# One rotation of four PSUM buffers for attention, in a hybrid encoder layer on one core

## The chip, the cores and the metric

The kernel runs on one core of one Trainium2 chip. The core has five engines with an instruction queue each: TensorE (PE in the profile, with its weight loads as PEld), VectorE (DVE), ScalarE (ACT), GpSimd (POOL) and SyncE (SP), which here only issues transfers. Matrix products and transposes run on TensorE and land in PSUM, which has eight banks of 2 KB for each of 128 partitions; a full tile of 128 x 512 float32 fills one. VectorE and ScalarE read PSUM. The metric is the device time of one execution in microseconds; less is better.

## The reference

The kernel computes one layer of an encoder on 2048 positions of width 1024, in float32. The input is normalised (RMS norm) and projected by `w_in` into 11 slots of 256 columns. Four mixers read them, each with a gate, and `w_out` projects their outputs back onto the residual:

```
h = rmsnorm(x, norm_g)
a_u, a_v, a_g, b_q, b_k, b_v, b_g, c_in, c_g, d_q, d_g = split(h @ w_in, 11)
y_a = chunked_spatial_gating(a_u, a_v, ...) * silu(a_g)     # 128x128 mixing per chunk
y_b = neighbourhood_attention(b_q, b_k, b_v, ...) * silu(b_g) # windows of 8 x 16 on a 32 x 64 grid, 4 heads
y_c = fourier_mixing(c_in, fn_w) * silu(c_g)                  # 2-D DFT, real part, then a linear map
y_d = memory_attention(d_q, rmsnorm(mem), ...) * silu(d_g)    # 256 memory tokens, 4 heads
x   = x + concat(y_a, y_b, y_c, y_d) @ w_out
```

## The kernel before

**Products.** To keep float32 accuracy at the faster rate, each operand is split into a high and a low half (`hi`, `lo`, type float32r): ScalarE copies the value with rounding (L506 and others), VectorE or GpSimd subtracts (L507 and others). A product then takes three matmuls, high by high, high by low and low by high. So a tile that leaves PSUM through `evac_split` is read twice: by the cast (L506) and, after that, by the subtraction (L507).

**Order.** TensorE's order is the program's: it is built by `drive`, which runs a filler (the projections, later the output projection) and squeezes in steps of other tasks as they fall due by a clock of costs that `mm` and `tr` add up. The instructions of the other engines and the transfers are ordered by Tile's own scheduler when the program is built; `hp(8000)` raises the priority of what is issued under it. Tile also sets all waits. On the chip every engine's queue runs in order.

**PSUM.** Eight banks: four in the pool `ps_acc` for the projections' sums, two in `ps_sc` and two in `ps_mi`. A pool's tiles take its buffers in rotation, whichever became free first by the scheduler's reckoning. A tile's first matmul waits until the last reader of the buffer's earlier tile has ended.

**Who uses the two small pools.** `ps_sc` (tiles `sc`): scores of both attentions, the sums of the memory's keys and values (`mem_kv`, L442), the Fourier sums (`acc`, L743), and an extra projection at the start. `ps_mi` (tiles `mi`): all else. That is transposes of normalised q and k (`emit_T`, read by L506/L507, or by L389/L390 where k is scaled), transposes of P (L592, L902) and the products with v (L600, L915) of both attentions, chunk mixing (`do_a`, L653), the first products of the Fourier stage (`pa`, L747), its two tiny products `pu` of two columns each (L773), and small preparations (`constants_a`: the bias; `constants_c`: the matrices G; `bcast`: the transposed norm rstd).

**Attention.** `pipeline` interleaves units. In step n it issues the score of unit n, the transposes of unit n-2, and, where unit n-3 closes an item, that item's product with v. An item of the memory attention (`d_`) has one unit, so a step takes three tiles: a score, a transpose tile and a product. An item of the window attention (`b_`) has two units, so two steps take five tiles. Between them the driver puts projection matmuls. A score of the memory attention is read by the row maximum (L575) and then by two exponentials (L579); a score of the window attention by one VectorE operation that adds the bias and takes the maximum (L886). P is scaled by VectorE (L583, L891) before it is transposed.

**Stages in time.** Start, with c_in and d_q and the memory's keys and values, up to some 100 us; memory attention of the first half of the positions among projections; projections alone; the Fourier stage among projections of the second half, from 347 us on; window attention, memory attention of the second half and both again, among the last projections and the output projection, from 472 us on; the rest of the output projection to the end.

Of the kernel before, what the change touches and what calls it, by code (L numbers as in the profile page):

```python
# [47 lines left out]
class Kern:  # L48
    def __init__(self, ctx, tc, ins, out, dbg=None):
        self.tc = tc  # L50
        self.nc = tc.nc
        self.ins = ins
        self.out = out
        self.ctx = ctx
        self.dbg = dbg
        p = lambda name, bufs, **k: ctx.enter_context(tc.tile_pool(name=name, bufs=bufs, **k))
        self.const = p("const", 1)
        self.xw = p("xw", 32)
        self.raw = p("raw", 5)
# [225 lines left out]
    def bcast(self, h):  # L285
        nc = self.nc
        ps = self.ps_mi.tile([8, 128], F32, name="mi")
# [79 lines left out]
    def transpose_pairs(self, srcs):  # L367
        ps = self.ps_mi.tile([128, 512], F32, name="mi")
# [71 lines left out]
    def mem_kv(self):  # L440
        nc, I = self.nc, self.ins
        ps = [self.ps_sc.tile([128, 512], F32, name="sc") for _ in range(2)]  # L442
        for k in range(8):
            with self.hp(0):
# [12 lines left out]
                w = [wt[:, k % 2, 0], wt[:, k % 2, 1]]  # L457
# [16 lines left out]
        for t in range(2):  # L474
# [7 lines left out]
                                    in1=self.vm[:, t, :, 0:HD].bitcast(F32), op=ALU.subtract)  # L482
        self.head_norm(q)
# [4 lines left out]
    def mem_k(self, twice):  # L488
        nc = self.nc
        self.km = [self.c([128, 4, 256], f"km{i}", F32R) for i in range(2)]  # L490
        for pr in range(2):
            ps = self.ps_mi.tile([128, 2, 256], F32, name="mi")
# [73 lines left out]
    def d_score(self, h, b, pr, hh, dq, o, ctx):  # L566
        nc = self.nc
        dqr = dq.bitcast(F32R)
        sc = self.ps_sc.tile([128, 512], F32, name="sc")
# [17 lines left out]
    def d_trans(self, h, b, pr, hh, dq, o, ctx):  # L587
# [4 lines left out]
        pt = self.ps_mi.tile([128, 2, 256], F32, name="mi")  # L592
# [5 lines left out]
    def d_pv(self, h, b, pr, hh, dq, o, ctx):  # L598
        PT = ctx["PT"][:, hh]
        pv = self.ps_mi.tile([128, 256], F32, name="mi")  # L600
# [9 lines left out]
    def constants_a(self):  # L610
# [10 lines left out]
        ps = self.ps_mi.tile([128, 512], F32, name="mi")  # L621
# [11 lines left out]
    def do_a(self, h, u, ps):  # L633
# [17 lines left out]
        for b in range(2):  # L651
            with self.hp(8000):
                ps2 = self.ps_mi.tile([128, 2, 2, 128], F32, name="mi")  # L653
# [10 lines left out]
    def constants_c(self):  # L664
# [7 lines left out]
        ps = self.ps_mi.tile([128, 4, 128], F32, name="mi")  # L672
# [3 lines left out]
        for pr in range(2):  # L676
            for i in range(2):
                nc.vector.tensor_copy(out=self.Gc[i][pr], in_=ps[:, pr * 2 + i, :])

    def fft(self, pool):  # L680
        nc, I = self.nc, self.ins
        for pr in range(2):
# [19 lines left out]
        for ty in range(4):  # L702
# [40 lines left out]
            acc = [self.ps_sc.tile([128, 512], F32, name="sc") for _ in range(2)]  # L743
            abs_ = {}
            for j in range(5):
                if j < 4:
                    pa = self.ps_mi.tile([128, 512], F32, name="mi")  # L747
# [24 lines left out]
            for pr, al in enumerate(als):  # L772
                pu = self.ps_mi.tile([128, 512], F32, name="mi")  # L773
                self.mm(pu[:, 0:2], self.Gc[0][pr], al[:, 2:4], True, True)
                nc.vector.tensor_copy(out=ucol[:, pr, :], in_=pu[:, 0:2])
# [12 lines left out]
            else:  # L788
                for pr in range(2):
# [14 lines left out]
                    nc.sync.dma_start(out=self.O[4 + pr][ty // 2], in_=z)  # L804
        self.done.add("fft")
# [65 lines left out]
    def b_score(self, pool, kv, qq, R, head, cb, ui, rb, gs, ctx):  # L871
# [5 lines left out]
        sc = self.ps_sc.tile([128, 512], F32, name="sc")  # L877
# [16 lines left out]
    def b_trans(self, pool, kv, qq, R, head, cb, ui, rb, gs, ctx):  # L894
# [7 lines left out]
        pt = self.ps_mi.tile([128, 4, 128], F32, name="mi")  # L902
# [6 lines left out]
    def b_pv(self, vt, R, head, cb, units, ctx):  # L909
# [5 lines left out]
        pv = self.ps_mi.tile([128, 2, 2, 128], F32, name="mi")  # L915
# [87 lines left out]
    def proj(self, h, *which):  # L1003
# [4 lines left out]
        for i, w in enumerate(which):  # L1008
            ps = []
            if i:  # L1010
                ps = [self.ps_sc.tile([128, 512], F32, name="sc") for _ in range(2)] + \
                     [self.ps_mi.tile([128, 512], F32, name="mi") for _ in range(2)]
            pss.append(ps)
            gens.append(self.slot(h, cs[w], w in self.NATURAL, ps, 1 if len(which) > 1 else 2))
# [32 lines left out]
    def main(self, P, es):  # L1047
# [7 lines left out]
        warm = self.ps_mi.tile([128, 512], F32, name="mi")  # L1055
# [51 lines left out]
    def run(self):  # L1107
# [6 lines left out]
        with tc.manual_schedule(engines={mybir.EngineType.PE}):  # L1114
            with ExitStack() as es:
# [4 lines left out]
                self.att = P("att", 2)  # L1120
                self.drive(self.main(P, es))

# [97 lines left out]
```

## Time and profile before

| | |
|---|---|
| median of 3 runs | 886.07 us (886.05 to 886.48) |
| the profiled execution | 886.93 us |
| its span, first to last instruction | 884.7 us |
| TensorE busy | 854.8 us, 97% of the span |
| VectorE, ScalarE, GpSimd busy | 516.5, 407.4 and 302.7 us |
| granted TensorE clock, mean | 0.993 of full speed |

Busy times are of one profiled execution. The profile names an instruction by its source line; most matmuls go through two helpers, so L135 is any matmul and L139 any transpose, and the tile (`mi`, `sc`, `acc`) tells which. Idle time of an engine is put down to what ended it.

### The profile page before, as it was taken

To read this page: it belongs to the slowest core of one execution; us is meant where nothing else is said; L and a number is where in the kernel's file an instruction comes from. 1 tells how busy PE (TensorE), PEld (TensorE's weight loads), DVE (VectorE), ACT (ScalarE), POOL (GpSimd) and SP (SyncE) were. 2 spreads that over 40 slices of the span, in tenths; PEclk is the share of its full clock that TensorE was granted. 3 is DMA by queue.
4 is the path that set the end of the run, shared out by engine and by line. 5 is a ranking of instruction groups with operands and counts; after the bars stand their busy time and mean duration, and the time that the engine had idled before them with its cause. 6 is when DMAs were issued, how large, how long until landed. Compare 5 with 4: busy or idle time off the path is not lost.

```text
span 884.7 us, 13646 instructions
## 1 busy us (share of the span) xinstructions
PE 854.8 (97%) x4448; PEld 714.5 (81%) x4448; DVE 516.5 (58%) x1104; ACT 407.4 (46%) x930; POOL 302.7 (34%) x329
## 2 busy tenths in 40 slices
PE   8999999999899999999999899999999999999998
PEld 7987788888688878787789788788877888878886
DVE  4345565487532646774444875776898877743331
ACT  5674354466732524443324544656775444521110
POOL 2136321155132213561231733442656333221110
PEclk9999999999999999999999999999999999999999
DMA  8958543455942653559668897864688987546662
GB/s 259 343 190 254 168 133 121 115 142 147 263 141 96 214 179 84 154 171 269 180 217 277 270 279 234 266 214 139 194 289 245 334 245 215 175 141 197 215 198 74
DMA packets 147462, 177.88 MB, mean 201 GB/s; under 512 B 29232, under 2 KB 105152, under 8 KB 147392
## 3 DMA queue, kind: packets, MB, share of 16 engines
q1 hardware_dynamic: 145104, 170.33, 62.1%
q0 software_dynamic: 1728, 6.29, 2.5%
q8 instruction: 35, 0.57, 0.3%
q10 hardware_dynamic: 560, 0.40, 0.2%
q14 instruction: 35, 0.29, 0.1%
HBM read 132.92 MB, written 44.05 MB: 200 GB/s over the span
## 4 chain that ended last, share of the span: by engine, by line
PE 67%; DMA 7%; DVE 6%; POOL 3%; issue 3%; ACT 2%; SPq 0%; DVEq 0%; POOLq 0%; ACTq 0%
PE acc L135 53%; PE mi L135 5%; PE sc L135 5%; PE mi L139 4%; DMA G<-st 2%; POOL hss L113 1%; DMA nat<-in_x 1%; DMA O<-sa_o 1%; DMA raw<-in_xT 1%; DMA qq<-QB 1%; DMA raw<-in_w_in 1%; DVE nat L364 1%; DVE PT L507 1%; DVE P L891 1%; DVE st L390 1%
## 5 line engine op out<-in xcount | busy, mean ns | idle before, releaser
L135 PE MATMUL acc<-hilo 128*128 128x512 f32 (+1 forms) x2880 | 709.9, 390 | 5.4 <-DVE nat L351 1.5
L135 PEld LDWEIGHTS acc<-hilo 128*128 128x128 f32 x2880 | 511.1, 189 | 96.7 <-ACT nat L353 1.6
L207 POOL TENSOR_TENSOR hilo<-raw,hilo 128x512 fp32r<-128x512 f32 x52 | 69.5, 1339 | 181.1 <-ACT hilo L205 160.6
L219 POOL TENSOR_TENSOR hilo<-raw,hilo 128x512 fp32r<-128x512 f32 x32 | 42.9, 1342 | 118.1 <-ACT hilo L217 94.6
L217 ACT CAST hilo<-raw 128x512 fp32r<-128x512 f32 x64 | 39.7, 621 | 75.7 <-PE acc L135 67.8
L953 POOL TENSOR_TENSOR nat<-nat 128x256 f32<-128x256 f32 x39 | 31.3, 805 | 104.2 <-DMA nat<-O 73.1
L507 DVE TENSOR_TENSOR PT<-mi,PT 128x512 fp32r<-128x512 f32 (+2 forms) x96 | 61.2, 637 | 8.1 <-ACT PT L506 8.1
L139 PE MATMUL mi<-ident,P 128*128 128x128 f32 (+1 forms) x352 | 54.6, 274 | 8.4 <-DVE PT L507 6.8
L139 PEld LDWEIGHTS mi<-ident,P 128*128 128x128 f32 (+1 forms) x352 | 42.2, 136 | 24.1 <-DVE PT L507 10.8
L959 ACT CAST hilo<-nat 128x256 fp32r<-128x256 f32 x64 | 25.7, 407 | 77.0 <-PE acc L135 67.3
L506 ACT CAST PT<-mi 128x512 fp32r<-128x512 f32 (+2 forms) x96 | 52.1, 542 | 18.9 <-PE mi L139 18.6
L888 ACT ACTIVATE P<-P,smx 128x288 f32<-128x288 f32 (+1 forms) x64 | 39.8, 622 | 40.3 <-DVE smx L886 40.1
L205 ACT CAST hilo<-raw 128x512 fp32r<-128x512 f32 x51 | 31.5, 619 | 48.3 <-PE acc L135 33.9
L219 DVE TENSOR_TENSOR hilo<-raw,hilo 128x512 fp32r<-128x512 f32 x32 | 23.7, 741 | 40.0 <-ACT hilo L217 34.1
L113 POOL TENSOR_TENSOR hss<-hss,mhalf 128x8 f32<-128x8 f32 x25 | 43.3, 1736 | 1.5
L891 DVE TENSOR_SCALAR P<-P,smx 128x288 f32<-128x288 f32 (+1 forms) x64 | 41.3, 645 | 1.9
L960 DVE TENSOR_TENSOR hilo<-nat,hilo 128x256 fp32r<-128x256 f32 x64 | 29.8, 474 | 21.4 <-ACT hilo L959 21.4
L579 ACT ACTIVATE P<-sc,smx 128x256 f32<-128x256 f32 x64 | 29.7, 469 | 23.4 <-DVE smx L575 23.2
L331 DVE TENSOR_TENSOR st<-acc,rbc 128x512 f32<-128x512 f32 x32 | 21.9, 683 | 30.2 <-PE acc L135 29.4
L928 POOL TENSOR_TENSOR ob<-tmp 64x128 f32<-64x128 f32 x64 | 30.3, 492 | 26.4 <-DVE tmp L924 25.4
L886 DVE CUSTOM_DVE_ANT_0 P<-sc,bt 128x288 f32<-128x288 f32 (+1 forms) x64 | 35.5, 555 | 3.1 <-PE sc L135 1.3
L126 DVE SCALAR_TENSOR_TENSOR hilo<-raw,gcol,hilo 128x512 fp32r<-128x512 f32 x32 | 25.2, 796 | 18.6 <-ACT hilo L125 18.2
(158 smaller groups left out, 1039.7 us busy)
## 6 DMA issues: line engine op xcount, KB each, us to landing
raw<-in_w_in SPq DMA_DIRECT2D x119, 256.0 KB
raw<-in_xT SPq DMA_DIRECT2D x32, 256.0 KB
nat<-in_x SPq DMA_DIRECT2D x32, 256.0 KB
G<-st SPq DMA_DIRECT2D x32, 256.0 KB
nat<-G SPq DMA_DIRECT2D x64, 128.0 KB
st<-in_x SPq DMA_DIRECT2D x32, 256.0 KB
out_y<-st SPq DMA_DIRECT2D x31, 256.0 KB
tab<-in_dft_s POOLq DMA_DIRECT2D x12, 512.0 KB, 4.3
```

What stands on the lines that cost most here:

```text
L113: nc.gpsimd.tensor_tensor(out=out, in0=out, in1=self.mhalf[:, :n], op=ALU.pow)
L135: self.nc.tensor.matmul(out=out, lhsT=lhsT, rhs=rhs, start=start, stop=stop, **k)
L139: self.nc.tensor.transpose(out=out, in_=in_, identity=self.ident)
L205: nc.scalar.copy(out=w[0], in_=raw)
L207: eng.tensor_tensor(out=w[1], in0=raw, in1=w[0].bitcast(F32), op=ALU.subtract)
L217: nc.scalar.copy(out=w[0], in_=raw)
L219: eng.tensor_tensor(out=w[1], in0=raw, in1=w[0].bitcast(F32), op=ALU.subtract)
L506: self.nc.scalar.copy(out=hi, in_=src)
L507: (eng or self.nc.vector).tensor_tensor(out=lo, in0=src, in1=hi.bitcast(F32), op=ALU.subtract)
L886: nc.vector.tensor_tensor_reduce(out=P[:, :n], in0=sc[:, :n], in1=bt[:, :n], op0=ALU.add, op1=ALU.min, scale=-1.0, scalar=3e38, accum_out= ...
L888: nc.scalar.activation(out=P[:, :n], in_=P[:, :n], func=AF.Exp, bias=sm[:, 1:2], scale=-1.0, accum_out=sm[:, 2:3])
L891: nc.vector.tensor_scalar(out=P[:, :n], in0=P[:, :n], scalar1=sm[:, 3:4], scalar2=None, op0=ALU.mult)
```

## The change

`psum()` closes the two small pools and opens others in their banks: either the two of two buffers, or one of four, which both names then stand for. It is called with the shared form at the end of `mem_kv`, with the split form at the start of the Fourier stage, and with the shared form again at its end. The new pools wait tile by tile (`reuse_waits="tile"`). All tiles of the small pools go by it, so `emit_T` and `do_a` too take from the four while these are shared. The two tiny products of the Fourier stage write columns 0:2 and 2:4 of one tile and are copied at once. The addition of the bias and the four copies of G are issued at higher priority.

```
-        self.ps_sc = p("ps_sc", 2, space=PSUM)
-        self.ps_mi = p("ps_mi", 2, space=PSUM)
+        self.pst = None
+
+    def psum(self, shared):
+        if self.pst is not None:
+            self.pst.close()
+        self.pst = ExitStack()
+        p = lambda name, bufs: self.pst.enter_context(
+            self.tc.tile_pool(name=name, bufs=bufs, space=PSUM, reuse_waits="tile"))
+        if shared:
+            self.ps_sc = self.ps_mi = p("ps_w", 4)
+            self.nsc = self.nmi = "w"
+        else:
+            self.ps_sc, self.ps_mi = p("ps_sc", 2), p("ps_mi", 2)
+            self.nsc, self.nmi = "sc", "mi"
...
     def mem_kv(self):
...
+        self.psum(True)
         self.head_norm(q)
...
     def constants_a(self):
...
-        nc.vector.tensor_tensor(out=self.bias2, in0=pv, in1=self.bias2, op=ALU.add)
+        with self.hp(8000):
+            nc.vector.tensor_tensor(out=self.bias2, in0=pv, in1=self.bias2, op=ALU.add)
...
     def constants_c(self):
...
-        for pr in range(2):
-            for i in range(2):
-                nc.vector.tensor_copy(out=self.Gc[i][pr], in_=ps[:, pr * 2 + i, :])
+        with self.hp(8000):
+            for pr in range(2):
+                for i in range(2):
+                    nc.vector.tensor_copy(out=self.Gc[i][pr], in_=ps[:, pr * 2 + i, :])

     def fft(self, pool):
         nc, I = self.nc, self.ins
+        self.psum(False)
...
-            for pr, al in enumerate(als):
-                pu = self.ps_mi.tile([128, 512], F32, name="mi")
-                self.mm(pu[:, 0:2], self.Gc[0][pr], al[:, 2:4], True, True)
-                nc.vector.tensor_copy(out=ucol[:, pr, :], in_=pu[:, 0:2])
+            if als:
+                pu = self.ps_mi.tile([128, 512], F32, name=self.nmi)
+                for pr, al in enumerate(als):
+                    self.mm(pu[:, pr * 2:pr * 2 + 2], self.Gc[0][pr], al[:, 2:4], True, True)
+                nc.vector.tensor_copy(out=ucol.rearrange("p a b -> p (a b)"), in_=pu[:, 0:4])
...
+        self.psum(True)
         self.done.add("fft")
...
                 self.att = P("att", 2)
+                self.psum(False)
                 self.drive(self.main(P, es))
+                self.pst.close()
```

Everywhere else the change only replaces a tile's name, `name="sc"` by `name=self.nsc` and `name="mi"` by `name=self.nmi`.

## Rows read from the trace of the kernel before

**Rows 1.** The page's first part: each engine's busy time, share and instructions

```profile
PE 854.8 (97%) x4448; PEld 714.5 (81%) x4448; DVE 516.5 (58%) x1104; ACT 407.4 (46%) x930; POOL 302.7 (34%) x329
```

**Rows 2.** Waits of TensorE: waiter, releaser, us in total, times, longest

```profile
PE mi L139 <- DVE PT L507: 8.1, 6, 1.9
```

**Rows 3.** Timeline, first half's memory attention: start, us, instruction, [idle before <-releaser]

```profile
220.93 0.46 ACT L579 ACTIVATE P<-sc,smx 128x256 f32<-128x256 f32 x1
...
223.56 0.66 PE L139 MATMUL mi<-ident,nat 128*128 128x128 f32 x4 [1.31 <-DVE PT L507]
...
225.63 0.74 PE L135 MATMUL mi<-PT,vm 128*128 128x256 f32 x4 [1.42 <-DVE st L390]
...
234.65 0.63 PE L139 MATMUL mi<-ident,P 128*128 128x128 f32 x4 [1.41 <-DVE st L390]
```

**Rows 4.** Timeline, Fourier stage

```profile
366.49 0.15 DVE L775 COPY ucol<-mi 128x2 f32<-128x2 f32 x1
...
366.69 0.38 PE L135 MATMUL mi<-al,G 128*128 128x2 f32 x2 [1.36 <-DVE ucol L775]
...
368.18 1.09 PE L139 MATMUL mi<-ident,nat 128*128 128x128 f32 x4 [0.30 <-DVE ucol L775]
```

**Rows 5.** Windows: length, engines' busy us (x), granted clock, DMA share, GB/s

```profile
367.00:372.00 5.00, 4.70 (x17) 3.63 (x17) 3.22 (x10) 1.80 (x5) 0.00 (x0) 0.66 0.63 204
```

**Rows 6.** Timeline, start of the window attention

```profile
474.94 0.44 PE L135 MATMUL sc<-kk,qq 128*128 128x384 f32 x1 [1.08 <-DVE smx L886]
...
475.79 0.37 DVE L891 TENSOR_SCALAR P<-P,smx 128x288 f32<-128x288 f32 x1
```

**Rows 7.** Timeline, window attention, a little later

```profile
494.19 0.35 DVE L891 TENSOR_SCALAR P<-P,smx 128x288 f32<-128x288 f32 x1
...
497.21 0.68 DVE L507 TENSOR_TENSOR PT<-mi,PT 128x512 fp32r<-128x512 f32 x1
...
497.94 0.53 PE L139 MATMUL mi<-ident,P 128*96 128x128 f32 x3 [1.31 <-DVE PT L507]
...
501.98 1.08 PE L135 MATMUL mi<-PT,vt 128*128 128x512 f32 x5 [1.68 <-DVE PT L507]
```

**Rows 8.** Timeline of TensorE, three stalls of the later attention

```profile
600.14 0.66 PE L139 MATMUL mi<-ident,P 128*128 128x128 f32 x4 [0.87 <-DVE PT L507]
...
674.08 0.66 PE L139 MATMUL mi<-ident,P 128*128 128x128 f32 x4 [0.80 <-DVE PT L507]
...
775.32 0.66 PE L139 MATMUL mi<-ident,P 128*128 128x128 f32 x4 [1.88 <-DVE PT L507]
```

**Rows 9.** Timeline, second half's window attention

```profile
663.99 0.64 PE L139 MATMUL mi<-ident,P 128*96 128x128 f32 x4 [1.94 <-DVE PT L507]
...
665.67 0.74 DVE L960 TENSOR_TENSOR hilo<-nat,hilo 128x256 fp32r<-128x256 f32 x2
```

**Rows 10.** Windows around it: PE, PEld, DVE, ACT, POOL busy, clock, DMA share

```profile
590.00:690.00 100.00, 96.16 (x504) 79.75 (x503) 80.27 (x174) 67.19 (x164) 53.17 (x54) 0.98 0.73 230
664.00:669.00 5.00, 4.87 (x19) 3.63 (x19) 3.96 (x11) 3.68 (x9) 4.89 (x5) 0.66 0.94 291
```

**Rows 11.** Timeline of TensorE, a product of the window attention

```profile
566.88 1.09 PE L135 MATMUL mi<-PT,vt 96*128 96x512 f32 x5 [0.62 <-DVE PT L507]
```

**Rows 12.** Timeline, the start of the kernel

```profile
70.05 0.66 PE L139 MATMUL mi<-ident,nat 128*128 128x128 f32 x4 [1.02 <-DVE G L678]
...
71.72 0.47 DVE L453 SCALAR_TENSOR_TENSOR P<-dq,gmcol,P 128x256 fp32r<-128x256 f32 x1
...
72.59 0.27 PE L139 MATMUL mi<-ident,rstd 128*8 128x128 f32 x1 [1.19 <-DVE bias L624]
```

**Rows 13.** Timeline, second half's memory attention

```profile
593.43 0.63 PE L135 MATMUL sc<-km,dq 128*128 128x256 f32 x4
...
597.95 0.63 PE L135 MATMUL sc<-km,dq 128*128 128x256 f32 x4
...
598.08 0.46 ACT L579 ACTIVATE P<-sc,smx 128x256 f32<-128x256 f32 x1
```

More of the change, by code (lines that the diff above doesn't have):

```diff
@@ L286, in bcast @@
         nc = self.nc
-        ps = self.ps_mi.tile([8, 128], F32, name="mi")
+        ps = self.ps_mi.tile([8, 128], F32, name=self.nmi)
         self.tr(ps, self.rstd[h])
@@ L367, in transpose_pairs @@
     def transpose_pairs(self, srcs):
-        ps = self.ps_mi.tile([128, 512], F32, name="mi")
+        ps = self.ps_mi.tile([128, 512], F32, name=self.nmi)
         for pr in range(2):
@@ L441, in mem_kv @@
         nc, I = self.nc, self.ins
-        ps = [self.ps_sc.tile([128, 512], F32, name="sc") for _ in range(2)]
+        ps = [self.ps_sc.tile([128, 512], F32, name=self.nsc) for _ in range(2)]
         for k in range(8):
@@ L491, in mem_k @@
         for pr in range(2):
-            ps = self.ps_mi.tile([128, 2, 256], F32, name="mi")
+            ps = self.ps_mi.tile([128, 2, 256], F32, name=self.nmi)
             for hh in range(2):
@@ L568, in d_score @@
         dqr = dq.bitcast(F32R)
-        sc = self.ps_sc.tile([128, 512], F32, name="sc")
+        sc = self.ps_sc.tile([128, 512], F32, name=self.nsc)
         for j in range(2):
@@ L591, in d_trans @@
         PT = ctx["PT"][:, hh]
-        pt = self.ps_mi.tile([128, 2, 256], F32, name="mi")
+        pt = self.ps_mi.tile([128, 2, 256], F32, name=self.nmi)
         for mt in range(2):
@@ L599, in d_pv @@
         PT = ctx["PT"][:, hh]
-        pv = self.ps_mi.tile([128, 256], F32, name="mi")
+        pv = self.ps_mi.tile([128, 256], F32, name=self.nmi)
         for mt in range(2):
@@ L620, in constants_a @@
         yield 12.0
-        ps = self.ps_mi.tile([128, 512], F32, name="mi")
+        ps = self.ps_mi.tile([128, 512], F32, name=self.nmi)
         pv = ps[:, 0:256].rearrange("p (a q) -> p a q", a=2)
         self.s_mix(pv, lnb)
-        nc.vector.tensor_tensor(out=self.bias2, in0=pv, in1=self.bias2, op=ALU.add)
+        with self.hp(8000):
+            nc.vector.tensor_tensor(out=self.bias2, in0=pv, in1=self.bias2, op=ALU.add)
         nc.vector.tensor_scalar(out=self.bias2, in0=self.bias2, scalar1=2.0, scalar2=None, op0=ALU.mult)
@@ L652, in do_a @@
             with self.hp(8000):
-                ps2 = self.ps_mi.tile([128, 2, 2, 128], F32, name="mi")
+                ps2 = self.ps_mi.tile([128, 2, 2, 128], F32, name=self.nmi)
                 for j in range(2):
@@ L671, in constants_c @@
         yield 10.0
-        ps = self.ps_mi.tile([128, 4, 128], F32, name="mi")
+        ps = self.ps_mi.tile([128, 4, 128], F32, name=self.nmi)
         for pr in range(2):
@@ L742, in fft @@
             yield 5.0
-            acc = [self.ps_sc.tile([128, 512], F32, name="sc") for _ in range(2)]
+            acc = [self.ps_sc.tile([128, 512], F32, name=self.nsc) for _ in range(2)]
             abs_ = {}
@@ L746, in fft @@
                 if j < 4:
-                    pa = self.ps_mi.tile([128, 512], F32, name="mi")
+                    pa = self.ps_mi.tile([128, 512], F32, name=self.nmi)
                     for pr in range(2):
@@ L876, in b_score @@
         gl = slice(r0 // 4 - (0, 3)[R], (r0 + nr) // 4 - (0, 3)[R])
-        sc = self.ps_sc.tile([128, 512], F32, name="sc")
+        sc = self.ps_sc.tile([128, 512], F32, name=self.nsc)
         q = qq[:, (rb - 2 * R) * 4 + cb, :]
@@ L901, in b_trans @@
         PT = ctx["PT"]
-        pt = self.ps_mi.tile([128, 4, 128], F32, name="mi")
+        pt = self.ps_mi.tile([128, 4, 128], F32, name=self.nmi)
         for s, gg in enumerate(gs):
@@ L914, in b_pv @@
         PT = ctx["PT"]
-        pv = self.ps_mi.tile([128, 2, 2, 128], F32, name="mi")
+        pv = self.ps_mi.tile([128, 2, 2, 128], F32, name=self.nmi)
         mms = [(pv, units[0][1][s], PT[:ck, s]) for s in range(2)]
@@ L1010, in proj @@
             if i:
-                ps = [self.ps_sc.tile([128, 512], F32, name="sc") for _ in range(2)] + \
-                     [self.ps_mi.tile([128, 512], F32, name="mi") for _ in range(2)]
+                ps = [self.ps_sc.tile([128, 512], F32, name=self.nsc) for _ in range(2)] + \
+                     [self.ps_mi.tile([128, 512], F32, name=self.nmi) for _ in range(2)]
             pss.append(ps)
@@ L1054, in main @@
         self.constants_mem()
-        warm = self.ps_mi.tile([128, 512], F32, name="mi")
+        warm = self.ps_mi.tile([128, 512], F32, name=self.nmi)
         for i in range(18):
```

## The prediction, as it was put on record

> **What bounds the kernel now.** I read the page's first part first: TensorE counts as busy for 97% of the span, no other engine for more than 58% [rows 1]. So time can only be won where TensorE stands still, and next I read who it waits for. The largest entry is waits of transposes into `mi` (L139) for the second half of a split (L507 on VectorE), 8.1 us in 6 waits [rows 2]. A transpose doesn't read what L507 writes, it reads P or a projection. One that waits for L507 waits for a buffer: two `mi` tiles are alive, and neither has been read to its end. Products do read what L507 writes, so each of their waits has to be looked at. Third, I went through the timeline around each stall and asked: was the data there earlier, and would another buffer have been free?
>
> **The change, part by part.** No matmul is added, removed or moved: TensorE's order is the program's, written out by the driver, and the change leaves its costs as they are. VectorE loses one tiny copy of 0.15 us [rows 4], which is worth nothing by itself. What changes is which earlier tile a tile has to wait for, and VectorE's order in two places. The prices below are the idle time that the timeline prints behind a matmul.
>
> *Memory attention of the first half.* Three stalls of 1.31, 1.42 and 1.41 us [rows 3]. The first and third are transposes, so they wait for buffers. The second is a product; it waits for L390, which it never reads, so for a buffer too. At the first of them both score buffers had been read to the end, the last one by an exponential that ended at 220.93 + 0.46 = 221.39. Sharing four should remove all three: 4.1 us. What follows is projection work whose loads are released by buffers that TensorE frees, so I keep the whole amount.
>
> *Fourier stage.* The second tiny product waits 1.36 us for the copy of the first (L775), and the next transposes wait 0.30 us for the second copy [rows 4]. With one buffer for both no product waits. The transposes then need the one copy, which in the trace would be over at 366.49 + 0.15 = 366.64, while they start at 368.18 now. I take 1.5 of the 1.66 us. The stall has a second price: right behind it the granted clock is 0.66 over 5 us [rows 5], that is at its lower level (1.2 GHz) for most of them. Lost: 0.34 x 5 = 1.7 us. If TensorE doesn't stand still there, I expect no fall: 1.7 us more.
>
> *Start of the window attention.* The third score waits 1.08 us for a score buffer [rows 6]. Four buffers remove that, but next in line is a transpose of P, scaled from 475.79 on in 0.37 us, so ready at 476.16, however early the score is. I take 0, bound 1.1. A little later a transpose waits 1.31 us and a product 1.68 us [rows 7]. The product's own data was there at 497.21 + 0.68 = 497.89, four us before it started; it is held by a buffer. Both go: 3.0 us.
>
> *Later attention.* Three transposes wait 0.87, 0.80 and 1.88 us for a buffer [rows 8]. The first and third I take whole; at the second VectorE is late in general, so 0.6. A fourth waits 1.94 us, but the output projection behind it needs the halves that L960 writes from 665.67 on [rows 9], and VectorE is busy 80.27 of 100 us around there [rows 10]. If the transpose starts earlier, the projection stands still instead. I take 0.3 us (bounds 0 and 1.94), and no credit for the lower clock that follows (0.66 over 5 us [rows 10], 1.7 us again). Sum: 0.87 + 1.88 + 0.6 + 0.3 = 3.6. One product waits 0.62 us for L507 of its own unit [rows 11]: that is data, and it stays.
>
> *Higher priority for two sets of VectorE operations at the start.* Transposes wait 1.02 us for the copies of G, and the transpose of rstd 1.19 us for the bias [rows 12]. Earlier copies free both, but the product behind the second one, to the memory's keys and values, needs the half that L453 writes from 71.72 on in 0.47 us, so at 72.19; the transpose starts at 72.59. That makes 0.4 us to be won, bounds 0 and 2.2.
>
> *Switching pools* three times issues nothing. A tile of a new pool waits at most for the last reader of its bank; I take 0, and as upper bound one wait like that of [rows 11] each, 1.9 us.
>
> Together 4.1 + 1.5 + 1.7 + 3.0 + 3.6 + 0.4 = 14.3 us. Part of it will be given back: a TensorE that comes earlier meets VectorE's data where it met a buffer before. The nearest row for that is the product that waits for its own data [rows 11]; four more of these are 2.4 us (bounds: 0, and the 6.6 us of the window attention's two terms, which is the first rival). That leaves some 12 us. The sum is made against the span of 884.7 us and that execution's own 886.93, which lies 0.86 above the median of 886.07: 874.9 for such an execution, 874.0 for the median.
>
> The Trainium skill, Perfetto Trace Analysis, section Identifying Performance Opportunities, says that the same gap repeating on the engine that should be saturated can mean too little PSUM for the next tile. Read that way, all of these stalls would go, which is the second rival below. The trace agrees only in part: the stalls are scattered over 700 us, and in some of them VectorE's data is late as well [rows 9].
>
> **Rivals.** *VectorE is what is late (0.18).* In the window attention the buffers may only be the place where its lateness shows; the waits then go over to data. For it: 80 of 100 us busy [rows 10]. Against it: P of the first transpose in [rows 7] was ready at 494.19 + 0.35 = 494.54, 3.4 us before the transpose started. Left are the terms before the window attention: 4.1 + 1.5 + 1.7 + 0.4 = 7.7, so 878.4.
>
> *Everything goes (0.10).* 8.1 [rows 2] + 1.68 [rows 7] + 1.42 + 1.41 [rows 3] + 1.66 [rows 4] + 1.08 [rows 6] + 2.21 [rows 12] = 17.6, with twice 1.7 of lost clock 21.0: 865.1. Against it stands the order of data in [rows 6, 9, 12].
>
> *DMA takes the lead back (0.08).* In places the transfers are close to saturation (a share of 0.94 [rows 10]). If TensorE's lead ends there and only the last stall of [rows 8] counts, the gain is 1.9: 884.2, hardly to be told from no change. Against it: most loads wait for buffers that TensorE frees, so they move with it.
>
> *Slower (0.06): scores hold the rotation up.* A score tile is read until its second exponential ends. In the second half's memory attention that is from 593.43 to 598.08 + 0.46 = 598.54, 5.1 us [rows 13]. The next score comes at 597.95, so a step is 4.5 us. Now the score's buffer is needed again two steps later, after 9.0 us; in a rotation of four with three tiles to a step, after 4/3 steps, 6.0 us. The margin is 0.9 us. If a new order on VectorE and ScalarE makes these reads later than that, transposes and products wait for scores. Over 80 units (16 to the memory, 64 windows) it decides from 0.18 us each, which eats the 14.3; at 0.3 us the time is 886.07 + 24 - 14.3 = 895.8. In this way the change could also fail to do what it says: which buffer a tile gets is fixed when the program is built, and on the chip that one may be the late one.
> The Trainium skill, TensorE: Matmul & The Clock Gate, section A second HAM failure mode: psum-queue depth-cycling, tells of short idle times between groups that cycle through PSUM banks, and of a clock that falls between them. Here the lower clock stands behind two stalls [rows 5, 10], and the change makes stalls fewer; in the slow case it would add to the loss.
>
> **How the numbers follow.** Forecast 874.0 with a chance of 0.58 (868 to 877 for itself). The range for 8 in 10 is 866 to 881: it takes in VectorE's case, the bounds of the forecast's own terms and the near side of the fast one, and leaves out DMA's case, the slow one and the far ends. About 0.2%, 1.8 us, is what a measurement of this kernel can tell from no change. Faster has the forecast, VectorE's and the fast case and a part of DMA's: 0.88. Same: 0.06. Slower: 0.06.
>
> **What would show it.** Right: in the memory attention of the first half TensorE waits for no buffer; the copy of the tiny products is there once, with no lower clock behind it; TensorE's waits at shared tiles fall from 17.1 us (the 17.6 without the score, with the 0.62) to under 6. The step on VectorE is right if the output projection waits for L960 near where the fourth transpose waited. Wrong: waits of TensorE for readers of scores (L579, L886), waits for L507 before products in place of those before transposes, or new stretches at the lower clock.

## The result, and the profile after

The changed kernel takes 876.97 us (median of 6 runs, 874.57 to 879.69); the kernel before takes 886.28 in the same measurement. The ratio is 0.9896, 95% interval 0.987 to 0.9922: 9.3 us less, with 6.9 to 11.5 inside the interval. The forecast was 874.0, 12 us less, range 866 to 881. A second program whose instructions stand in the same order (the fourth experiment) gave 878.25, ratio 0.9913 (0.9883 to 0.9943).

The profiled execution took 879.69 us with a span of 877.5, the longest of the six; before's took 886.93 with 884.7. So the two traces differ by 7.2 us, and it is these 7.2 that can be followed. The first part of the page after, which answers to [rows 1]:

```profile
PE 852.0 (97%) x4448; PEld 713.3 (81%) x4448; DVE 515.3 (59%) x1103; ACT 407.6 (46%) x930; POOL 302.0 (34%) x329
```

TensorE runs the same 4448 matmuls in the same order, so each can be found in both traces. Its start before minus its start after is the *lead* at that place. The forecast column adds up the prediction's terms.

| after the stalls of | start before | start after | lead | forecast |
|---|---|---|---|---|
| the head (transpose of rstd) | 72.59 | 72.44 | 0.15 | 0.4 |
| first half's memory attention | 234.65 | 229.20 | 5.45 | 4.5 |
| the projection behind it | 247.44 | 246.00 | 1.44 | 4.5 |
| Fourier stage | 371.19 | 366.97 | 4.22 | 7.7 |
| start of the window attention | 504.64 | 497.84 | 6.80 | 10.7 |
| later attention | 775.32 | 765.90 | 9.42 | 14.3 |
| output projection | 858.75 | 851.36 | 7.39 | 12.0 |

Stage by stage the wins are not far from the forecast's (5.3, 2.8, 2.6 and 2.6 us where it had 4.1, 3.2, 3.0 and 3.6). The lead is lost in two places that the forecast didn't name: the third row and the last.

*First half.* Timeline of TensorE after. The first three rows answer to [rows 3]:

```profile
221.37 0.60 PE L151 MATMUL w<-ident,nat 128*128 128x128 f32 x4
221.72 0.72 PE L147 MATMUL w<-PT,vm 128*128 128x256 f32 x4
...
229.20 0.60 PE L151 MATMUL w<-ident,P 128*128 128x128 f32 x4
...
234.10 0.71 PE L147 MATMUL w<-PT,vm 128*128 128x256 f32 x4 [1.12 <-DVE st L402]
...
243.26 1.66 PE L147 MATMUL acc<-hilo 128*128 128x512 f32 x6 [1.14 <-DVE st L343]
246.00 1.19 PE L147 MATMUL acc<-hilo 128*128 128x512 f32 x4 [1.07 <-DVE st L343]
```

The three stalls of before have no bracket any more: no wait. They gave 1.47, 1.72 and 1.54 us of lead. Behind them stand three new ones, which cost 1.24, 1.39 and 1.38. The first is a product that never reads what L402 writes, so it waits for one of the four buffers. The other two are projection matmuls, which wait for an accumulator that the gate's evacuation (L343) has not read yet. Why that is late is seen on ScalarE and VectorE together (timeline, ScalarE first):

```profile
240.44 0.63 ACT L291 ACTIVATE nat<-nat 128x512 f32<-128x512 f32 x1 [1.45 <-DMA nat<-in_x]
240.98 0.19 ACT L291 ACTIVATION_READ_ACCUMULATOR nat<-nat 128x1 f32 x1
241.07 0.61 ACT L345 ACTIVATE st<-st 128x512 f32<-128x512 f32 x1
```

```profile
241.72 0.69 DVE L350 SCALAR_TENSOR_TENSOR st<-st 128x512 f32<-128x512 f32 x1 [1.34 <-ACT st L345]
242.51 0.69 DVE L343 TENSOR_TENSOR st<-acc,rbc 128x512 f32<-128x512 f32 x1
```

Read it backwards from 243.26. L343 ended at 242.51 + 0.69 = 243.20. On VectorE it stands behind L350, which waits for a tanh (L345). On ScalarE that tanh stands behind a square of the second half's statistics (L291), which waits 1.45 us for its load. Nothing in this chain needs the statistics; they only stand ahead in the queue.

The squares could not come much earlier, because their loads did not. Windows of 15 us, before and after, and the last square of each:

```profile
230.00:245.00 15.00, 13.59 (x71) 11.26 (x70) 7.65 (x14) 12.00 (x31) 2.01 (x2) 1.00 1.03 286
230.00:245.00 15.00, 12.67 (x59) 9.70 (x56) 8.37 (x14) 11.98 (x31) 2.60 (x2) 1.00 1.03 290
```

```profile
247.34 0.62 ACT L279 ACTIVATE nat<-nat 128x512 f32<-128x512 f32 x1
246.57 0.62 ACT L291 ACTIVATE nat<-nat 128x512 f32<-128x512 f32 x1
```

The share of the DMA engines is 1.03 in both kernels. TensorE was 5.45 us ahead at 229 us, the last square is 0.77 us ahead.

*Fourier stage* (timeline, and a window of 5 us as in [rows 5]), answers to [rows 4]:

```profile
363.64 0.51 PE L147 MATMUL mi<-al,G 128*128 128x2 f32 x4
...
365.31 0.66 PE L151 MATMUL mi<-ident,nat 128*128 128x128 f32 x4 [0.36 <-DVE ucol L792]
```

```profile
364.00:369.00 5.00, 4.64 (x23) 3.60 (x23) 4.26 (x13) 2.21 (x5) 0.58 (x1) 1.00 0.85 248
```

All four matmuls of the two products stand in one group (before, two per tile), no wait between them, and a granted clock of 1.00 where it was 0.66.

*Window attention.* Timeline of TensorE, the places of [rows 6] and [rows 7]:

```profile
469.40 0.34 PE L147 MATMUL w<-kk,qq 128*128 128x384 f32 x1
...
472.13 0.50 PE L151 MATMUL w<-ident,P 128*96 128x128 f32 x3 [1.51 <-DVE P L909]
...
492.06 0.49 PE L151 MATMUL w<-ident,P 128*96 128x128 f32 x3
...
494.25 1.04 PE L147 MATMUL w<-PT,vt 128*128 128x512 f32 x5
...
497.84 0.64 PE L151 MATMUL w<-ident,P 128*96 128x128 f32 x4 [0.79 <-DVE PT L520]
```

The third score no longer waits, and the next transpose waits for its scaled P instead (lead +1.31, then -1.37). The two stalls of [rows 7] are gone (+1.46, +1.85). A new one of 0.79 costs 0.94: what it waits for stands on VectorE behind a multiplication (L376) of 2.26 us.

*Later attention.* The places of [rows 8], then that of [rows 9] with VectorE's side, then the windows that answer to [rows 10]:

```profile
591.72 0.60 PE L151 MATMUL w<-ident,P 128*128 128x128 f32 x4
...
664.96 0.60 PE L151 MATMUL w<-ident,P 128*128 128x128 f32 x4
...
765.90 0.60 PE L151 MATMUL w<-ident,P 128*128 128x128 f32 x4
```

```profile
653.69 0.64 PE L151 MATMUL w<-ident,P 128*96 128x128 f32 x4 [0.41 <-DVE P L909]
654.09 0.94 PE L147 MATMUL acc<-hilo 128*128 128x512 f32 x3
657.33 1.65 PE L147 MATMUL acc<-hilo 128*128 128x512 f32 x3 [2.29 <-DVE st L343]
```

```profile
656.60 0.68 DVE L343 TENSOR_TENSOR st<-acc,rbc 128x512 f32<-128x512 f32 x1
657.20 0.74 DVE L978 TENSOR_TENSOR hilo<-nat,hilo 128x256 fp32r<-128x256 f32 x2
```

```profile
590.00:690.00 100.00, 97.10 (x509) 81.07 (x507) 80.45 (x176) 64.75 (x155) 49.05 (x51) 0.98 0.72 228
655.00:660.00 5.00, 2.71 (x8) 2.29 (x8) 3.96 (x10) 3.99 (x9) 4.65 (x5) 0.70 0.95 308
```

The three transposes go (+1.02, +0.94, +2.13). The fourth stall moves from the transpose to the projection behind it (+1.58, then -1.83), with the lower clock still behind it.

*End.* The output projection, VectorE and TensorE:

```profile
826.42 0.43 DVE L971 TENSOR_TENSOR nat<-nat 128x256 f32<-128x256 f32 x1 [3.02 <-DMA nat<-O]
826.76 0.76 DVE L978 TENSOR_TENSOR hilo<-nat,hilo 128x256 fp32r<-128x256 f32 x2
827.43 2.48 DVE L1015 TENSOR_TENSOR st<-acc,st 128x512 f32<-128x512 f32 x4
```

```profile
828.26 3.91 PE L147 MATMUL acc<-hilo 128*128 128x512 f32 x16 [0.65 <-DVE st L1015]
```

The same shape as at 243 us: accumulators wait for the final additions (L1015), which stand on VectorE behind a gating product (L971) that waits 3.02 us for its load. Here it cost 0.72, at 851.36 once more 1.31. TensorE, which came earlier, met them; in the trace before it didn't wait there at all. How much this costs differs between executions: in the traces of the fourth, fifth and ninth experiments TensorE waits 1.0, 0.4 and 0.2 us for these additions.

### The profile page after: what moved, and what is told of

The parts are those of the page before. It is cut to its first block, busy times and chain, and to the rows that moved or that the text cites. A ratio compares the mean times of both kernels' runs of the same rounds, so it can differ in the third digit from the quotient of the medians.

```text
span 877.5 us, 13679 instructions
## 1 busy us (share of the span) xinstructions
PE 852.0 (97%) x4448; PEld 713.3 (81%) x4448; DVE 515.3 (59%) x1103; ACT 407.6 (46%) x930; POOL 302.0 (34%) x329
## 5 line engine op out<-in xcount | busy, mean ns | idle before, releaser
L971 POOL TENSOR_TENSOR nat<-nat 128x256 f32<-128x256 f32 x39 | 29.9, 767 | 105.1 <-DMA nat<-O 63.8
L520 DVE TENSOR_TENSOR PT<-w,PT 128x512 fp32r<-128x512 f32 (+2 forms) x96 | 61.2, 638 | 5.9 <-ACT PT L519 5.7
L519 ACT CAST PT<-w 128x512 fp32r<-128x512 f32 (+2 forms) x96 | 52.1, 542 | 17.2 <-PE w L151 16.8
L151 PE MATMUL w<-ident,P 128*128 128x128 f32 (+1 forms) x352 | 54.2, 273 | 2.7 <-DVE P L909 1.9
L151 PEld LDWEIGHTS w<-ident,P 128*128 128x128 f32 (+1 forms) x352 | 42.9, 136 | 16.4 <-issue 1.9
L978 DVE TENSOR_TENSOR hilo<-nat,hilo 128x256 fp32r<-128x256 f32 x64 | 32.6, 521 | 17.0 <-ACT hilo L977 17.0
L904 DVE CUSTOM_DVE_ANT_0 P<-w,bt 128x288 f32<-128x288 f32 (+1 forms) x64 | 35.5, 556 | 11.3 <-DMA bt<-in_bias 9.3
L909 DVE TENSOR_SCALAR P<-P,smx 128x288 f32<-128x288 f32 (+1 forms) x64 | 39.7, 621 | 1.9
L592 ACT ACTIVATE P<-w,smx 128x256 f32<-128x256 f32 x64 | 29.7, 469 | 21.4 <-DVE smx L588 21.2
L343 DVE TENSOR_TENSOR st<-acc,rbc 128x512 f32<-128x512 f32 x32 | 21.9, 684 | 29.5 <-PE acc L147 28.7
```

Source lines behind the costliest of these rows:

```text
L151: self.nc.tensor.transpose(out=out, in_=in_, identity=self.ident)
L519: self.nc.scalar.copy(out=hi, in_=src)
L520: (eng or self.nc.vector).tensor_tensor(out=lo, in0=src, in1=hi.bitcast(F32), op=ALU.subtract)
L904: nc.vector.tensor_tensor_reduce(out=P[:, :n], in0=sc[:, :n], in1=bt[:, :n], op0=ALU.add, op1=ALU.min, scale=-1.0, scalar=3e38, accum_out= ...
L909: nc.vector.tensor_scalar(out=P[:, :n], in0=P[:, :n], scalar1=sm[:, 3:4], scalar2=None, op0=ALU.mult)
L978: nc.vector.tensor_tensor(out=y[:, 1], in0=g, in1=y[:, 0].bitcast(F32), op=ALU.subtract)
```

## The experiments

Each says what it edits; "after" is the changed kernel. Times are medians with the ratio to the kernel before, measured beside it on the same chip. The before kernel's median was 885.2 to 886.7 in these measurements. The ratio is not simply that of the two medians: in the second experiment the medians give 0.9972, the ratio is 0.9987. The intervals reach 1.9 to 3.5 us to either side, more than the 1.8 us that the prediction took for what can be told from no change.

**One part alone: the shared buffer of the two tiny products.** The kernel before, with only this part of the change:

```diff
-            for pr, al in enumerate(als):
...
-                nc.vector.tensor_copy(out=ucol[:, pr, :], in_=pu[:, 0:2])
+            if als:
...
+                nc.vector.tensor_copy(out=ucol.rearrange("p a b -> p (a b)"), in_=pu[:, 0:4])
```

> The kernel before with one edit: the two tiny products of the Fourier stage share one buffer and one copy; the pools stay two and two. My theory: the 1.36 us wait at the second product goes, and with it the lower clock that followed it (1.7), so 2.8 to 3.2 us less: ratio 0.9965. Rival 1, the clock dip was not this wait's doing: only the wait goes, 1.4 us, ratio 0.9985. Rival 2, the work was hidden anyway: ratio 1.000. In the trace, theory: granted clock 1.00 from 366 to 372 us, where it was 0.66.

885.41 us, 0.9982 (0.9956 to 1.0009). By the time the theory (0.9965) and both rivals lie inside the interval. The windows say more:

```profile
224.00:232.00 8.00, 6.13 (x21) 5.02 (x22) 2.42 (x6) 4.42 (x11) 1.27 (x1) 0.61 0.71 219
...
366.00:372.00 6.00, 5.64 (x35) 4.70 (x34) 5.28 (x12) 2.44 (x6) 1.89 (x3) 1.00 0.70 216
```

The wait is gone and so is the lower clock behind it, but in this execution a longer stretch of lower clock stands at 224 to 232 us, behind the stalls of [rows 3], where the trace before had none. Whether the dip belongs to the stall of the Fourier stage, one trace of each kernel can't say; the ninth experiment comes back to this.

**The rotation in the first half only.** After without the call that shares the buffers again at the end of `fft`, and with the two copies and the priorities of before:

```diff
-        self.psum(True)
         self.done.add("fft")
```

> The four buffers in one rotation only between the end of the memory keys' projection and the start of the Fourier stage; everything else as before, the Fourier stage with its two copies, no higher priority. My theory, from the lead of the kernel after over the kernel before, matmul by matmul: the rotation wins 5.2 us by 229 us and 4.0 of these are given back between 234 and 246 us, where the accumulators are freed late because ScalarE's queue waits for data; 1.2 to 1.5 us less remain: ratio 0.9985. Rival, the 4.0 were a disturbance of one execution, not of the kernel: 4 to 5 us less, ratio 0.995.

883.17 us, 0.9987 (0.9961 to 1.0014): the interval holds the theory's 0.9985 and leaves out the rival's 0.995. The trace repeats after's: the three stalls give 4.73 us of lead, and the same three waits take 4.01 back:

```profile
235.51 0.71 PE L147 MATMUL w<-PT,vm 128*128 128x256 f32 x4 [1.48 <-DVE st L402]
...
244.30 1.66 PE L147 MATMUL acc<-hilo 128*128 128x512 f32 x6 [0.74 <-DVE st L343]
247.04 1.20 PE L147 MATMUL acc<-hilo 128*128 128x512 f32 x4 [1.08 <-DVE st L343]
```

So the loss belongs to the kernel, not to one execution.

**The rotation after the Fourier stage only.** The same without the calls in `mem_kv` and at the start of `fft`, and with the one behind it:

```diff
-        self.psum(True)
         self.head_norm(q)
...
-        self.psum(False)
```

> The four buffers in one rotation only after the Fourier stage; everything else as before. My theory: wins of 3.0 at the start of the window attention, 3.6 in the later attention, less what comes back as waits for data and for the output additions (about 3.5): about 3.5 to 4.5 us less: ratio 0.9955. Rival, the gains of the later stages hang on the first half's lead: under 2 us less, ratio 0.998 or more. With the parts adding up, the three kernels with one part each should give 1.4 + 3 + 4 = 8 to 9 us together, as much as the whole change did (9.3); less if they gain from one another.

884.41 us, 0.9977 (0.995 to 1.0004): theory (0.9955) and rival (0.998) both fit. The trace stands nearer to the theory: TensorE gains 5.2 us between 371 us and the end, about 1.4 of them from a dip at 665 us that did not come this time, though TensorE waits 2.29 us there again. The three parts by themselves give 0.9982 x 0.9987 x 0.9977 = 0.9946, the whole 0.9896 and 0.9913. That is 4.8 us for the parts, where 8 to 9 were expected, against 9.3 and 7.7. Whether the parts help one another stays open: the intervals overlap.

**Without the higher priority.** After, with bias and copies of G at normal priority.

```diff
-        with self.hp(8000):
-            nc.vector.tensor_tensor(out=self.bias2, in0=pv, in1=self.bias2, op=ALU.add)
+        nc.vector.tensor_tensor(out=self.bias2, in0=pv, in1=self.bias2, op=ALU.add)
```

> The kernel after without the higher priority on the four copies of G and the bias addition. My theory: they stand in the same place of VectorE's order either way, and the waits of 0.96 and 1.18 us behind them stay: same time as the kernel after, 877 us, ratio to before 0.990. Rival (the prediction's own term): the priority is worth 0.4 us or more: 877.4 us or more, the waits longer than 0.96 and 1.18.

878.25 us, 0.9913 (0.9883 to 0.9943). The order of instructions is the same on every engine with and without it, and the waits are 1.0 and 1.2 us. The priority does nothing.

**Statistics later, in one run.** After, with the first loads held until the first gate is done:

```diff
+                if k0 == 0 and cj == 1 and t == 1:
+                    self.late = self.c([128, 1], "late")
+                    nc.vector.tensor_copy(out=self.late, in_=th[:, 0:1])
...
-        self.stats(1)
+        self.stats(1, self.late)
```

> The kernel after, with the second half's statistics loaded later: a one-column copy of the first gate's last product goes into the five buffers before the loads, so that no square of L291 stands ahead of that gate's tanh in ScalarE's queue. My theory: the accumulator waits at 243.26 and 246.00 us (1.4 each beyond before's) and the wait at 234.10 (1.1) come from these squares, which wait for their data with the tanh queued behind them: 2 to 3.5 us less than after, so about 874 us, ratio to before 0.987, and in the trace accumulator waits behind L343 of under 1 us between 230 and 250. Rival 1, the store buffers that tanh needs are what is late: the waits stay, same time as after. Rival 2, the squares, now in one run, hold up the weights' casts behind them: waits of the same size come 10 to 20 us later.

876.20 us, 0.9883 (0.9844 to 0.9922). All three waits are gone (lead over after: 1.28, 1.34 and 1.38, together 4.0), as the theory says. The edit does two things at once, though: it takes the squares out of the queue, and their loads out of these 15 us (DMA share 0.68 from 230 to 245 us, 1.03 in after). So it shows that the statistics are the cause, while their place ahead of the tanh is read from the chain above. And something like rival 2 comes at the next gate, with a tanh and not a weights' cast behind the squares:

```profile
265.61 2.74 PE L147 MATMUL acc<-hilo 128*128 128x512 f32 x7 [2.78 <-DVE st L343]
```

Its tanh stood behind the last squares of the run, and a window of 264 to 269 us has a granted clock of 0.74. Nothing was left of the 4.0.

**One score buffer, three for the rest.** After, but

```diff
-            self.ps_sc = self.ps_mi = p("ps_w", 4)
-            self.nsc = self.nmi = "w"
+            self.ps_sc, self.ps_mi = p("ps_sc", 1), p("ps_mi", 3)
+            self.nsc, self.nmi = "sc", "mi"
```

> The kernel after, but where it has four buffers in one rotation this has one for the scores and three for transposes and products. Theory: what was short before was a third buffer for transposes and products, and now and then a second score's; a score buffer is held for some 4.5 to 5.1 us, so with one alone each next score waits for the exponentials of the one before: 5 to 40 us more than after, near or over the kernel before: ratio 0.995 to 1.03. Rival: scores are far enough apart, and three for the rest give nearly all: within 2 us of after, ratio 0.990 to 0.992.

889.42 us, 1.0041 (1.0018 to 1.0064): slower than before. Waits of TensorE:

```profile
PE sc L147 <- ACT P L592: 5.0, 5, 1.5
PE sc L147 <- DVE smx L904: 4.6, 4, 2.9
```

Scores now wait 9.6 us for the readers of the score before. So it isn't that transposes and products needed one more buffer than they had: the scores' second buffer is needed too, at other times.

**Three buffers in the rotation.**

```diff
-            self.ps_sc = self.ps_mi = p("ps_w", 4)
+            self.ps_sc = self.ps_mi = p("ps_w", 3)
```

> The kernel after with three buffers in the rotation instead of four. If what the rotation gives is only that any free buffer can be taken, three should cost little against two and two: theory, one score and three others are wanted at a time at the stalls of before, so with three the fourth waits again: the waits of 1.3 to 1.9 us per pair of heads come back and more of them; 5 to 20 us more than after, 882 to 897 us, ratio to before 0.995 to 1.012. Rival: under 2 us more than after, three are enough.

882.37 us, 0.9948 (0.992 to 0.9975), 5.4 more than after. Waits of TensorE:

```profile
PE w L151 <- DVE PT L520: 4.3, 4, 1.3
PE w L151 <- DVE st L402: 3.8, 1, 3.8
```

Buffer waits of transposes come back. But three in one rotation still beat four that are split two and two, by 3.9 us, and four split one and three by 7.1. Of after's 9.3 us, then, some 4 come with a rotation of three (the tiny products' part is in them) and 5.4 from having the fourth buffer in it.

**No gating product on VectorE.** After, with

```diff
-            mul = nc.vector if q > 4 and k % 2 else nc.gpsimd
+            mul = nc.gpsimd
```

> The kernel after, with every gating product of the output projection on GpSimd, none on VectorE. My theory: the accumulator waits of 0.7 at 828.26 and 1.1 to 1.3 at 851.36 come from L1015's additions queued on VectorE behind L971, which waits there for its load; without L971 in that queue both go: 2 us less than after, about 875 us, ratio to before 0.9875. Rival: the additions wait for the accumulators and x alone, and the waits stay, or come back as waits for L978 behind GpSimd's products (0.74 us each, where VectorE took 0.43): same time as after.

877.03 us, 0.989 (0.9854 to 0.9927): by the time no difference from after, though the interval holds the theory's 0.9875 too. In its trace TensorE waits nowhere from 800 us on, and it gains 0.90 and 1.33 us on after at the two places, as the theory says of after's trace. The same execution lost more than that earlier, mostly to clock dips at other places (mean granted clock 0.992, after's 0.995). That the gain is 2 us in other executions too is not shown.

**After with two tiny products in two buffers.**

```diff
-                nc.vector.tensor_copy(out=ucol.rearrange("p a b -> p (a b)"), in_=pu[:, 0:4])
+                nc.vector.tensor_copy(out=ucol[:, pr, :], in_=pu[:, 0:2])
```

and the tile inside the loop again.

> The kernel after with two buffers and two copies for the two tiny products of the Fourier stage, as before the change. Theory: the 1.4 us wait at the second product comes back, and with some chance the 1.7 us of lower clock that followed it: 1.5 to 3 us more than after, 878.5 to 880 us, ratio to before 0.992. Rival, the copy is hidden once the lead is there: same as after, 0.9896.

877.89 us, 0.9899 (0.9861 to 0.9937), 0.9 more than after; the interval holds both cases. Timeline and window:

```profile
364.53 0.38 PE L147 MATMUL mi<-al,G 128*128 128x2 f32 x2 [1.38 <-DVE ucol L791]
```

```profile
364.00:369.00 5.00, 4.17 (x21) 3.28 (x22) 3.94 (x12) 2.19 (x5) 0.00 (x0) 1.00 0.80 256
```

The wait is back with 1.38 us, as long as in [rows 4], and this time the clock behind it stays at 1.00. Three more kernels keep the two copies, those of the second, third and eleventh experiments. Their traces have the wait with 1.38, 1.36 and 1.40 us, and these windows behind it:

```profile
366.00:371.00 5.00, 4.71 (x24) 3.70 (x25) 3.36 (x10) 1.96 (x5) 0.00 (x0) 1.00 0.77 238
368.00:373.00 5.00, 4.53 (x22) 3.61 (x23) 3.58 (x12) 2.19 (x5) 0.00 (x0) 1.00 0.74 233
369.00:374.00 5.00, 4.27 (x21) 3.35 (x22) 3.85 (x12) 2.19 (x5) 0.00 (x0) 1.00 0.79 248
```

So of five traces with this stall only before's has the dip: the 1.7 us of clock can't be counted as part of its price.

**Statistics in three parts, and no gating product on VectorE.** After, with `mul = nc.gpsimd` and five squares behind the first gate, five behind the second, six behind the third, each part held by the last product of the gate before it:

```diff
-        self.stats(1)
+        self.stats(1, self.late, 0, 5)
...
+            if q == "d_g":
+                self.stats(1, self.late, 5, 10)
+            elif q == "b_g":
+                self.stats(1, self.late, 10, 16)
```

> The kernel after with two edits: the second half's statistics loaded and squared in three parts, five squares behind each of the first two gates and six behind the third, so that they stand between the gates in ScalarE's queue and before no tanh; and every gating product of the output projection on GpSimd. Theory: the three waits at 234 to 246 us (4.0 together) go and the 2.8 us that came with all squares in one run does not come; the waits of 2.0 us at 828 and 851 us go too: 5 to 6 us less than after, about 871.5 us, ratio to before 0.983. Rival: what is won is lost again at the next late part, as in the two edits by themselves: 875 to 877 us.

879.24 us, 0.992 (0.9891 to 0.9948): the rival. The waits at 234 to 246 us are gone, but the last squares now stand among the input's splits for the second half. Waits of TensorE from 300 to 320 us, and ScalarE there:

```profile
PE acc L147 <- DVE st L349: 4.8, 4, 1.9
```

```profile
302.74 1.44 ACT L137 ACTIVATE hilo<-raw,gcol 128x512 fp32r<-128x512 f32 x2 [2.93 <-DMA raw<-in_xT]
```

The last gate's evacuation (L349 here) is late behind splits that wait for loads, and the lead over after falls by 6.9 us between 246 and 319 us, most of it in these waits.

**The same two edits on the kernel before.**

> The kernel before, with the same two edits and none of the change. Theory: it runs late enough in both places for them to be hidden (no accumulator wait at 230 to 250 nor in the output projection): same time as before, ratio 0.999 to 1.001; so what they win exists only with the change. Rival: they win by themselves 2 us or more, ratio 0.9975 or less.

885.91 us, 0.9996 (0.9976 to 1.0017): same time. Not quite for the reason given: ScalarE without squares freed the buffers of [rows 3] earlier (two of the three stalls gone, lead 3.2), and the waits of the last gate then took more than that back, as in the run above. In the output projection neither kernel waits.

**Statistics in two parts.** After, with ten squares behind the first gate and six behind the second, and `mul = nc.gpsimd`:

```diff
-        self.stats(1)
+        self.stats(1, self.late, 0, 10)
         for q in ("d_g", "b_g", "c_g"):
             yield from self.proj(0, q)
+            if q == "d_g":
+                self.stats(1, self.late, 10, 16)
```

> The kernel after with two edits: the second half's statistics in two parts, ten squares behind the first gate and six behind the second, so that they are over before the input's splits for the second half; and every gating product of the output projection on GpSimd. Theory: the three waits at 234 to 246 us go (4.0 us; the three-part version took them away too, and lost 5 to 6 us at 305 to 315 us, where its last squares had made the splits' loads late), that loss does not come, and the waits of 2.0 us at 828 and 851 us go: TensorE 5 to 6 us ahead of after at the end, about 871.5 us, ratio to before 0.983. Rival: squares and splits still collide somewhere, and 875 to 878 us remain, ratio 0.988 or more.

871.86 us, 0.9839 (0.9818 to 0.986): 14.1 us less than before and 5.1 less than after's median, and the intervals of the two ratios lie apart. TensorE where after had its three waits (timeline):

```profile
233.59 0.64 PE L147 MATMUL w<-PT,vm 128*128 128x256 f32 x4
...
235.94 14.24 PE L147 MATMUL acc<-hilo 128*128 128x512 f32 x62
```

One unbroken row of 62 matmuls. The lead over after is 3.23 us at 246 us and 5.66 at the end, 2.1 of it from the two places in the output projection. This placement of the squares was not tried on the kernel before, so it is not shown that all of the 5.1 us need the change: in the experiment before this one, 3.2 us of lead stood at 247 us without it.

## Why the prediction was right or wrong

**Direction and mechanism: right.** TensorE stood still for buffers because of how they were divided, not for lack of them. The seven large stalls that the prediction wanted gone, three in the first half, two at the start of the window attention and two of the three in [rows 8] that it took whole, are gone. TensorE's waits at shared tiles fell from 17.1 to 5.5 us (0.8 and 1.0 for L520, 0.4 for `ucol`, 1.0 and 1.2 in the head, 1.1 for L402), which the prediction wanted under 6. Not in the 5.5 are 1.9 us of waits for P (L909) and 0.4 for a load of v: these are waits for data, which the trace before doesn't have; with them it is 7.8. The Trainium skill, Perfetto Trace Analysis, section Identifying Performance Opportunities, says that a gap that repeats can mean too little PSUM for the next tile. The runs agree only in part: no PSUM was added, and four buffers gave 886, 889 and 877 us, depending on who may take which.

**First half, 4.1 us: the step that failed.** The stalls gave 4.7, but "so I keep the whole amount" was wrong: 4.0 came back within 17 us. The prediction thought of the loads that wait for TensorE, and not of the accumulators: an earlier TensorE needs them earlier, and the engines that read them out did not get earlier. They stood behind squares whose loads wait for buffers that ScalarE frees (SyncE's issues of them wait 6.9 us for L291 between 222 and 248 us), while the transfers run at a DMA share of 1.03. One of the three new waits is for a shared buffer, too, where it had wanted none. The second and fifth experiments and the last show the cause. The 2.4 us that the prediction took off for all that is "given back" were too few for this one place; with the 2.0 of the output projection 6.0 came back in this trace. That is the term of its sum that was mis-sized most.

**Fourier stage, 1.5 + 1.7: right in this trace, 2.8 measured; the second term right by chance.** The wait fell by 1.36 and the next transposes still wait 0.36 (0.30 before; the forecast left 0.16 of the 1.66), since the one copy stands behind a 0.66 us instruction on VectorE. The dip went, but four other traces have the stall without the dip (ninth experiment).

**Start of the window attention, 3.0: 2.6 measured.** The third score's stall turned into a wait for P of the same size, as forecast. The two others gave 3.3, and VectorE took 0.9 back a few us later.

**Later attention, 3.6: 2.6 measured.** The three stalls gave 4.1, more than the 3.35 taken for them. Two products, at 692.00 and 707.11, now wait for a load and for L520 and lost 1.5, where the prediction had counted such waits in its 2.4. The 1.94 us moved to the projection with the lower clock behind it, as forecast, but the line was misnamed: L343 ends at 657.28 and the matmul starts at 657.33, so it waits for an accumulator of the last gate, not for the half that L978 (L960 before) writes next to it.

**Head, 0.4: nothing.** The scheduler already had these operations where the priority would put them.

**Output projection: not foreseen, 2.0 lost.** It is the first half's mistake a second time, and the eighth and last experiments remove it. The size is that of one execution; other traces lose less there.

**The rivals.** *VectorE is what is late* (878.4) lies nearer to 876.97 than the forecast does, but its reason failed: the window attention's gain did come. The time lies between the two because the gains came nearly as forecast and more was given back. *Everything goes* (865.1) did not come: waits for data took the place of some of the buffer waits. *DMA takes the lead back* (884.2) had the wrong price, but its mechanism has a part in the first half's loss: against it the prediction had set that most loads move with TensorE, and the loads for the squares didn't. Of the *slower* rival, three buffers in rotation are the case with one buffer less: the waits that came back there are for L520 and L402, most of them before transposes; none is for a score's reader. With four, no score or transpose waits for one either.

## What to carry to other kernels

A buffer wait that is removed makes the engine earlier everywhere behind it. Follow that lead to the next resource that another engine has to free, here the accumulators, and look in that engine's queue for an instruction that waits for a load and has nothing to do with it. Clearing two such queues was worth 5.1 us on top of the change's 9.3, but only where the moved work collides with nothing new: two of three placements of the same squares lost what they had won.
Before buffers are moved from one use to another, let the two share them.

## What the runs showed of the hardware

Behind a short stall one trace says little of the clock. Five traces have the stall of 1.36 to 1.40 us in the Fourier stage; over 5 us behind it the granted clock was 0.66 in one program and 1.00 in the four others. Near 660 us, where the fourth transpose and the projection behind it wait, the dip came more often: of ten traces with 1.7 to 2.8 us of waiting there, nine have a granted clock of 0.50 to 0.76 over the 5 us from the projection's start, and of four with 0.6 to 1.3 us none has a dip. Six executions of after list mean clocks from 0.995 to 1.0 and spans from 872.2 to 877.5 us. So one profile can't price a dip, and differences of 2 us between single executions say nothing of a kernel.
